# Three of eight gate groups per layer as seven block products, fed between 128-feature blocks

## The chip, the cores and the metric

The kernel runs on one core of a Trainium2 chip. The metric is device microseconds of one execution; lower is better. TensorE (PE) does the matrix products, VectorE (DVE) and ScalarE (ACT) the element-wise work, SyncE (SP) and GpSimd (POOL) issue transfers.

## The reference

Two layers of a decoder trunk over 256 positions of 2048 features. In each layer four branches (pooling, latent attention, gated convolution, cross-attention into memory) are projected to 2048 features and merged by sigmoid gates that are themselves a projection of the normed input `h`:

```python
proj = h @ w_in[l]
(pv, pz, cq, ckv, kr, mz, cb, cc, cx, cz, xq, xz, gpre) = jnp.split(proj, split_points, axis=-1)
y_pool = pool_mixer(pv, pool_w[l], pool_scale[l]) * jax.nn.silu(pz)
...
y_conv = conv_mixer(cb, cc, cx, conv_w[l]) * jax.nn.silu(cz)
...
gates = jax.nn.sigmoid((gpre + gate_b[l]).astype(jnp.float32)).astype(x.dtype).reshape(B, S, N_BRANCH, D_MODEL)
merged = gates[:, :, 0] * (y_pool @ w_branch[l, 0])
merged = merged + gates[:, :, 1] * (y_mla @ w_branch[l, 1])
...
x = x + merged @ w_out[l]
```

All arrays are float32. The gate projection `gpre` is 256 x 2048 times 2048 x 8192, in each layer.

## The kernel before

Every matrix operand is split into two float32r parts, `hi` (rounded) and `lo` (the rest), and a product is the sum of hi*hi, hi*lo and lo*hi. Weights come in chunks of 128 x 1024 numbers (512 KB): `wchunks` (L293) issues the transfer into `raw` on SP's queue (L303), ACT rounds it to `hi` (L304), DVE subtracts to get `lo` (L305). There are four buffers of `raw` and three each of `hi` and `lo`; `tc.high_priority(AHEAD)` puts these three steps ahead of other work that is ready.

Two loops use the chunks. `tm_block` (L308) holds 128 positions of an operand as the stationary side and streams 512 output features: twelve products of 512 columns a chunk (L317, L318, L319), 96 for a gate block of 512 features (K = 2048), into one two-bank `acc` tile. `fm_block` (L326) holds 128 features of the weights and streams the operand: its hi and lo parts together are 512 columns (L333), and the lo weights take 256 columns (L336). Its two 512-column results are added in halves by `fm_sum` (L339), an ACT copy and a DVE addition. PSUM has eight banks: three `acc` tiles of two, and two `ms` tiles of one.

The order inside a layer is written out by hand: attention first (`SEQUENCE`), then `gates` for the latent branch, the pooling branch, `gates` for memory, the convolution branch, and `gates` for pooling and convolution. `gates` (L809) goes over four blocks of 512 features: a gate block, bias (L818) and sigmoid (L819), the branch projection (48 products), multiplication (L825) and addition into `merged` (L826), which stays in on-chip memory for the whole layer. The pooling and convolution branches are `fm_block`s over `pv`, `pz`, `cc`, `cx`, `cb`, `cz` (256 features at a time), and DVE work between. The scheduler fixes each engine's order ahead of time and may put a later instruction that is ready ahead of one that waits.

Of the kernel before, what the change touches and what calls it, by code (L numbers as in the profile page):

```python
# [10 lines left out]
F32 = mybir.dt.float32  # L11
# [11 lines left out]
CK = 2  # L23
D = 2048
S = 256
DEPTH = 2
KT = D // P
# [33 lines left out]
def weight_plan():  # L61
# [7 lines left out]
    def fm(name):  # L69
        for b in range(4):  # L70
            add("in", OFF[name] + 256 * b, 256, 4, KT)

# [38 lines left out]
def tile_hybrid_trunk(  # L111
# [43 lines left out]
    x1d = ctx.enter_context(tc.tile_pool(name="dr", bufs=1, space=bass.MemoryType.DRAM)).tile([P, 2, D], F32, name="x1d")  # L155
# [170 lines left out]
    def fm_block(rhs, l, name, c0):  # L326
# [10 lines left out]
        return ps  # L337

# [160 lines left out]

    def silu_tile():  # L500
        return t4("z")[:, :1024].rearrange("p (n s) -> p n s", n=4)

    def silu_block(h, l, c0):
        z = silu_tile()
        for i in range(2):
            silu_half(z, i, h, l, c0)
        return z
# [226 lines left out]
    def pool_branch(l, vec, h):  # L734
        mixed = []
        for b in range(2):
            for i in range(2):
                ps = fm_block(h, l, "in", OFF["pv"] + 512 * b + 256 * i)
# [4 lines left out]
                fm_sum(v[:, :, 16:], ps)  # L743
# [35 lines left out]
    def conv_branch(l, vec, h):  # L779
        ys = []  # L780
        for b in range(2):
            cc = t4("cc")[:, :1024].rearrange("p (n s) -> p n s", n=4)
            for i in range(2):
                ps = fm_block(h, l, "in", OFF["cc"] + 512 * b + 256 * i)
                fm_sum(cc[:, 2 * i : 2 * i + 2, :], ps)
            u = t4("u")[:, :1032].rearrange("p (n s) -> p n s", n=4)
            nc.gpsimd.memset(u[:, :, :2], 0.0)
            for i in range(2):
                ps = fm_block(h, l, "in", OFF["cx"] + 512 * b + 256 * i)
                sl = slice(2 * i, 2 * i + 2)  # L790
                fm_sum(u[:, sl, 2:], ps)
# [8 lines left out]
            for i in range(2):  # L800
                ps = fm_block(h, l, "in", OFF["cb"] + 512 * b + 256 * i)
                sl = slice(2 * i, 2 * i + 2)
                fm_sum(bb[:, sl, :], ps)
                V.tensor_tensor(y[:, sl, :], y[:, sl, :], bb[:, sl, :], ALU.mult)
            sz = silu_block(h, l, OFF["cz"] + 512 * b)
# [3 lines left out]
    def gates(l, h, ys, branch, merged, first, last):  # L809
# [178 lines left out]
```

## Time and profile before

| | |
|---|---|
| median of 3 runs | 2513.04 us (2512.74 to 2514.82) |
| the profiled execution | 2512.52 us |
| its span in the trace | 2510.7 us |
| PE, PEld, DVE, ACT busy | 2498.8, 2110.1, 1538.0, 1249.1 us |
| bytes moved | 484.22 MB, mean 193 GB/s |

In the profile's rows a time is in microseconds unless marked ns; an `L` number is a line of the kernel, of a helper where several places share it; `out<-in` names tiles. A PE row's duration is the length of one product from start to drained end; products overlap, so the rate is read from the starts. PEld is the loading of the stationary side.

### The profile page before, as it was taken

Reading aid. Unit: us, or ns where it says so; the run is one execution under the profiler, and the core shown is the slowest. Engines: PE = TensorE matmul, PEld = TensorE weight load, DVE = VectorE, ACT = ScalarE, POOL = GpSimd, SP = SyncE. Lnnn points to the kernel's source line nnn. Section 1 sums busy time; section 2 is a strip of 40 time slices with the busy share of each in tenths; the row PEclk is TensorE's granted clock in tenths of the full one; section 3 lists DMA queues with packets and bytes.
Section 4 is the critical chain, followed back from the end, with each engine's and each line's share of the span. In section 5 each row is a group of like instructions: output and inputs, shape, how many; then the busy total and the mean of one; then the engine's idle time right before and its main releaser. Section 6 shows DMA issues by size and latency. Waiting matters only on the chain.

```text
span 2510.7 us, 32447 instructions
## 1 busy us (share of the span) xinstructions
PE 2498.8 (100%) x12402; PEld 2110.1 (84%) x12402; DVE 1538.0 (61%) x2132; ACT 1249.1 (50%) x1707; POOL 1.6 (0%) x16
## 2 busy tenths in 40 slices
PE   8999999999999999999999999999999999999999
PEld 7888888888888888888888888888888888888887
DVE  6767775566556665556474577755765566555554
ACT  7556674445444444445454566744444444444443
POOL 0000000000000000000000000000000000000000
PEclk9999999999999999999999999999999999999999
DMA  8665436655665566656655654366556655566565
GB/s 320 204 200 165 147 126 195 201 192 192 202 199 188 186 225 200 202 195 232 218 185 169 200 166 137 128 202 204 188 193 201 197 190 185 197 200 202 192 229 162
DMA packets 143677, 484.22 MB, mean 193 GB/s; under 512 B 16161, under 2 KB 17185, under 8 KB 143521
## 3 DMA queue, kind: packets, MB, share of 16 engines
q1 hardware_dynamic: 142800, 481.06, 58.9%
q8 instruction: 97, 1.59, 0.2%
q10 hardware_dynamic: 720, 1.09, 0.1%
q14 instruction: 60, 0.48, 0.1%
HBM read 477.89 MB, written 4.19 MB: 192 GB/s over the span
## 4 chain that ended last, share of the span: by engine, by line
PE 97%; DVE 1%; ACT 1%; DMA 0%; issue 0%; SPq 0%; DVEq 0%; ACTq 0%
PE acc L319 22%; PE acc L318 22%; PE acc L317 22%; PE acc L333 19%; PE acc L336 9%; PE ms L707 1%; PE ms L706 1%; PE ms L354 1%; DVE lo L305 0%; PE ms L555 0%; ACT hi L304 0%; PE ms L557 0%; PE ms L556 0%; PE acc L323 0%; DMA row<-in_x_dram 0%; PE ms L726 0%
## 5 line engine op out<-in xcount | busy, mean ns | idle before, releaser
L305 DVE TENSOR_TENSOR lo<-raw,hi 128x1024 fp32r<-128x1024 f32 (+2 forms) x884 | 1062.3, 1202 | 857.8 <-ACT hi L304 857.3
L304 ACT CAST hi<-raw 128x1024 fp32r<-128x1024 f32 (+2 forms) x884 | 914.6, 1035 | 1165.8 <-PE acc L319 794.4
L317 PE MATMUL acc<-hi,op 128*128 128x512 f32 (+2 forms) x2496 | 963.5, 386 | 5.6 <-ACT op L396 5.6
L318 PE MATMUL acc<-lo,op 128*128 128x512 f32 (+2 forms) x2496 | 959.3, 384 | 0.7 <-DVE lo L305 0.6
L319 PE MATMUL acc<-hi,op 128*128 128x512 f32 (+2 forms) x2496 | 958.9, 384 | 0.1
L333 PE MATMUL acc<-op,hi 128*128 128x512 f32 x2048 | 563.9, 396 | 0.0
L317 PEld LDWEIGHTS acc<-hi,op 128*128 128x128 f32 x2496 | 469.3, 188 | 93.9 <-ACT op L396 6.2
L318 PEld LDWEIGHTS acc<-lo,op 128*128 128x128 f32 x2496 | 469.5, 188 | 90.7 <-DVE lo L305 1.9
L319 PEld LDWEIGHTS acc<-hi,op 128*128 128x128 f32 x2496 | 469.1, 188 | 91.1 <-DVE op L397 0.7
L333 PEld LDWEIGHTS acc<-op,hi 128*128 128x128 f32 x2048 | 351.1, 189 | 47.9 <-issue 1.3
L336 PEld LDWEIGHTS acc<-op,lo 128*128 128x128 f32 x2048 | 314.8, 189 | 42.5
L336 PE MATMUL acc<-op,lo 128*128 128x256 f32 x2048 | 328.8, 282 | 0.0
L818 DVE TENSOR_TENSOR g<-acc,gb 128x1024 f32<-128x1024 f32 x32 | 39.2, 1224 | 12.7 <-PE acc L319 12.7
L341 ACT COPY fmt<-acc 128x512 f32<-128x512 f32 x72 | 41.5, 579 | 2.1 <-PE acc L336 2.1
L819 ACT ACTIVATE g<-g 128x1024 f32<-128x1024 f32 x32 | 34.0, 1062 | 6.7 <-DVE g L818 6.7
L825 DVE TENSOR_TENSOR g<-g,acc 128x1024 f32<-128x1024 f32 x24 | 29.3, 1222 | 9.9 <-PE acc L319 9.9
L826 DVE TENSOR_TENSOR merged<-merged,g 128x1024 f32<-128x1024 f32 x24 | 29.3, 1219 | 0.0
L498 DVE TENSOR_TENSOR z<-z,sg 128x512 f32<-128x512 f32 x32 | 22.1, 689 | 11.5 <-ACT sg L497 11.4
L197 ACT ACTIVATE junk<-acc 128x256 f32<-128x256 f32 (+2 forms) x68 | 25.3, 371 | 2.4 <-PE acc L319 1.5
L517 ACT ACTIVATE sm<-sm,smx,rqs 128x128 f32<-128x128 f32 (+1 forms) x32 | 17.3, 540 | 17.0 <-DVE smx L515 16.8
L497 ACT ACTIVATE sg<-z 128x512 f32<-128x512 f32 x32 | 20.2, 630 | 8.8 <-DVE z L342 8.6
L342 DVE TENSOR_TENSOR z<-acc,fmt 128x512 f32<-128x512 f32 x32 | 21.9, 684 | 1.6 <-ACT fmt L341 1.6
(197 smaller groups left out, 976.9 us busy)
## 6 DMA issues: line engine op xcount, KB each, us to landing
raw<-in_weights_dram SPq DMA_DIRECT2D x836, 512.0 KB, 4.0
raw<-in_weights_dram SPq DMA_DIRECT2D x32, 288.0 KB, 2.8
gb<-in_gate_b_dram SPq DMA_DIRECT2D x32, 256.0 KB, 4.2
raw<-in_weights_dram SPq DMA_DIRECT2D x16, 384.0 KB, 3.2
mt<-in_memT_dram SPq DMA_DIRECT2D x14, 256.0 KB, 6.0
row<-in_mem_dram SPq DMA_DIRECT2D x4, 512.0 KB, 8.4
row<-in_x_dram SPq DMA_DIRECT2D x4, 512.0 KB, 7.2
xt<-in_xT_dram SPq DMA_DIRECT2D x8, 256.0 KB, 5.6
```

What stands on the lines that cost most here:

```text
L304: A.copy(hi[:, :m], raw[:, :m])
L305: V.tensor_tensor(lo[:, :m], raw[:, :m], hi[:, :m].bitcast(F32), ALU.subtract)
L317: T.matmul(ps[:, t, :n], hh, hi[:, k, :], start=kk == 0, stop=False)
L318: T.matmul(ps[:, t, :n], hh, lo[:, k, :], start=False, stop=False)
L319: T.matmul(ps[:, t, :n], hl, hi[:, k, :], start=False, stop=kk == kt - 1)
L333: T.matmul(ps[:, j, :], hi[:, k, n0 : n0 + P], o, start=k0 + k == 0, stop=False)
L336: T.matmul(ps[:, j, :S], lo[:, k, n0 : n0 + P], o, start=False, stop=k0 + k == kt - 1)
L341: A.copy(tmp, ps[:, :, S:])
L818: V.tensor_tensor(g, pg, gb.unsqueeze(1).broadcast_to([P, 2, 512]), ALU.add)
L819: A.activation(g, g, AF.Sigmoid)
L825: V.tensor_tensor(g, g, pb, ALU.mult)
L826: V.tensor_tensor(mg, mg, g, ALU.add)
```

## The change

Of the eight pairs of gate blocks in a layer (four branches, two pairs of 1024 features), three, the two of pooling and the first of convolution (`SEVEN`), are computed by `seven`. It treats each of eight K slices of 256 as a 2 x 2 block product (two row halves of 128 positions, two K halves, two feature halves of 512) and forms seven block products from sums of blocks (Strassen's scheme, in Winograd's form) in place of eight; each is again three PE products of 512 columns. The seven results accumulate in seven PSUM banks, all three `acc` tiles and one `ms`, over the eight slices. The sums of operand blocks are made once per layer by `operand_sums`, the sums of weight blocks for every slice in place in `raw`, on DVE.

`seven` is a generator that yields after each product. `fine_block`, which takes the place of `fm_block` in the pooling and convolution branches, covers 128 features in one `ms` bank and first calls `pull(RATE)`, which runs on average 3.48 products of the stream (`RATE` = 160/46); the pooling projection pulls one product ahead of each of its results. The finished gates go to DRAM (`kept`) on POOL's queue and come back in `gates`. `merged` becomes four tiles in DRAM (`sums`), written and read on POOL's queue, since its buffer holds the operand sums. `hi` and `lo` get five buffers each, and the area for POOL's transfer descriptors shrinks. `gates` for memory now comes ahead of the pooling branch; pooling and convolution follow each other, with the stream between their blocks.

```diff
+SCRATCH = 1024
+FINE = ("pv", "pz", "cc", "cx", "cb", "cz")
 D = 2048
 S = 256
 DEPTH = 2
+SEVEN = [(0, 0), (0, 1), (2, 0)]
+RATE = (56 * len(SEVEN) - 8) / 46
...
     def fm(name):
-        for b in range(4):
-            add("in", OFF[name] + 256 * b, 256, 4, KT)
+        if name in FINE:
+            for b in range(8):
+                add("in", OFF[name] + 128 * b, 128, 8, KT)
+        else:
+            for b in range(4):
...
-            add("in", OFF["gate"] + bi * D + 512 * e, 512, 2, KT)
+            if (bi, e // 2) not in SEVEN:
+                add("in", OFF["gate"] + bi * D + 512 * e, 512, 2, KT)
+            elif e % 2 == 0:
+                add("in", OFF["gate"] + bi * D + 512 * e, 1024, 1, KT)
             add(f"br{bi}", 512 * e, 512, 2, 8)
...
+    dr = ctx.enter_context(tc.tile_pool(name="dr", bufs=1, space=bass.MemoryType.DRAM))
+    x1d = dr.tile([P, 2, D], F32, name="x1d")
+    sums = [dr.tile([P, 2, 512], F32, name=f"sums{e}") for e in range(4)]
+    kept = {(bi, 2 * ep + i): dr.tile([P, 2, 512], F32, name=f"kept{bi}{ep}{i}") for bi, ep in SEVEN for i in range(2)}
...
-            hi = wp.tile([P, 1024], F32R, tag="hi", name=nm("hi"), bufs=3)
-            lo = wp.tile([P, 1024], F32R, tag="lo", name=nm("lo"), bufs=3)
+            hi = wp.tile([P, 1024], F32R, tag="hi", name=nm("hi"), bufs=5)
+            lo = wp.tile([P, 1024], F32R, tag="lo", name=nm("lo"), bufs=5)
...
+    stream, owed = [], [0.0]
+
+    def pull(n):
+        owed[0] += n
+        while stream and owed[0] >= 1:
+            owed[0] -= 1
+            done = next(stream[0], True)
+            if done:
+                stream.pop(0)
+                break
+
...
+    def fine_block(rhs, l, c0):
+        pull(RATE)
+        ps = ms()
+        for k0, nk, kt, n, hi, lo in wchunks(l, "in", c0):
+            for k in range(nk):
+                o = rhs[(k0 + k) // 2][:, k % 2].rearrange("p a s -> p (a s)")
+                T.matmul(ps, hi[:, k, :], o, start=k0 + k == 0, stop=False)
+            for k in range(nk):
+                o = rhs[(k0 + k) // 2][:, k % 2, 0, :]
+                T.matmul(ps[:, :S], lo[:, k, :], o, start=False, stop=k0 + k == kt - 1)
+        return ps
+
+    def fine_sum(dst, ps):
+        tmp = t2("fmt")[:, :S]
+        A.copy(tmp, ps[:, S:])
+        V.tensor_tensor(dst, ps[:, :S], tmp, ALU.add)
+
...
+    def operand_sums(h, u, sx):
+        def run():
+            o = h[u]
+            w = t4("sw")
+            f = w[:, :512].rearrange("p (f s) -> p f s", f=4)
+            d = w[:, 512:1024].rearrange("p (f s) -> p f s", f=4)
+            a, b = slice(0, P), slice(P, S)
+            of = o.bitcast(F32)
+            V.tensor_tensor(d[:, 0:2, :], of[:, 0, :, b], of[:, 1, :, b], ALU.add)
+            V.tensor_tensor(d[:, 2:4, :], of[:, 0, :, a], of[:, 0, :, b], ALU.subtract)
+            V.tensor_tensor(f[:, 0:3:2, :], d[:, 0:3:2, :], d[:, 1:4:2, :], ALU.add)
+            V.tensor_tensor(f[:, 1, :], f[:, 0, :], of[:, 0, 0, a], ALU.subtract)
+            V.tensor_tensor(f[:, 1, :], f[:, 1, :], of[:, 0, 1, a], ALU.subtract)
+            V.tensor_tensor(f[:, 3, :], of[:, 1, 0, a], f[:, 1, :], ALU.subtract)
+            V.tensor_tensor(f[:, 3, :], f[:, 3, :], of[:, 1, 1, a], ALU.add)
+            q = sx[u // 4][:, u % 4]
+            A.copy(q[:, 0], f)
+            V.tensor_tensor(q[:, 1], f, q[:, 0].bitcast(F32), ALU.subtract)
+
+        return run
+
+    def seven(l, bi, ep, h, sx):
+        c0 = bi * D + 1024 * ep
+        off = plan["in", OFF["gate"] + c0][0]
+        a0, a1, a2, a3 = acc(), acc(), acc(), ms()
+        bank = {1: a0[:, 0, :], 6: a0[:, 1, :], 7: a1[:, 0, :], 5: a1[:, 1, :], 3: a2[:, 0, :], 2: a2[:, 1, :], 4: a3}
+        left, right = slice(0, 512), slice(512, 1024)
+        for u in range(8):
+            o, q = h[u], sx[u // 4][:, u % 4]
+            form = {
+                "A11": [o[:, 0, a, 0:P] for a in range(2)], "A12": [o[:, 1, a, 0:P] for a in range(2)],
+                "A22": [o[:, 1, a, P:S] for a in range(2)],
+            }
+            for i in range(4):
+                form[f"S{i + 1}"] = [q[:, a, i, :] for a in range(2)]
+
+            def product(i, name, pair, cols):
+                lh, (hi, lo) = form[name], pair
+                T.matmul(bank[i], lh[0], hi[:, cols], start=u == 0, stop=False)
+                T.matmul(bank[i], lh[0], lo[:, cols], start=False, stop=False)
+                T.matmul(bank[i], lh[1], hi[:, cols], start=False, stop=u == 7)
+
+            def pair():
+                hi = wp.tile([P, 1024], F32R, tag="hi", name=nm("hi"), bufs=5)
+                return hi, wp.tile([P, 1024], F32R, tag="lo", name=nm("lo"), bufs=5)
+
+            def lower(x, raw, cols):
+                V.tensor_tensor(x[1][:, cols], raw[:, cols], x[0][:, cols].bitcast(F32), ALU.subtract)
+
+            ra, rb = (wp.tile([P, 1024], F32, tag="raw", name=nm("raw"), bufs=4) for _ in range(2))
+            with tc.high_priority(AHEAD):
+                for i, r in enumerate((ra, rb)):
+                    at = off + P * 1024 * (2 * u + i)
+                    nc.sync.dma_start(r, weights[l, at : at + P * 1024].rearrange("(p m) -> p m", p=P))
+                x = pair()
+                A.copy(x[0][:, left], ra[:, left])
+                lower(x, ra, left)
+            product(1, "A11", x, left)
+            yield False
+            both = slice(0, 1024)
+            with tc.high_priority(AHEAD):
+                x = pair()
+                A.copy(x[0], rb)
+                V.tensor_tensor(ra[:, left], ra[:, right], ra[:, left], ALU.subtract)
+                V.tensor_tensor(ra[:, right], rb[:, right], ra[:, right], ALU.subtract)
+                lower(x, rb, both)
+            product(3, "S4", x, right)
+            yield False
+            product(2, "A12", x, left)
+            yield False
+            with tc.high_priority(AHEAD):
+                x = pair()
+                A.copy(x[0], ra)
+                V.tensor_tensor(rb[:, right], rb[:, right], ra[:, left], ALU.subtract)
+                V.tensor_tensor(rb[:, left], rb[:, right], rb[:, left], ALU.subtract)
+                lower(x, ra, both)
+            product(5, "S1", x, left)
+            yield False
+            product(7, "S3", x, right)
+            yield False
+            with tc.high_priority(AHEAD):
+                x = pair()
+                A.copy(x[0], rb)
+                lower(x, rb, both)
+            product(6, "S2", x, right)
+            yield False
+            product(4, "A22", x, left)
+            if u < 7:
+                yield False
+        c, u3 = t2("c"), t2("u3")
+        g = [t4("g")[:, :1024].rearrange("p (t c) -> p t c", t=2) for _ in range(2)]
+        A.copy(c, bank[1])
+        V.tensor_tensor(g[0][:, 0, :], c, bank[2], ALU.add)
+        V.tensor_tensor(c, c, bank[6], ALU.add)
+        V.tensor_tensor(u3, c, bank[7], ALU.add)
+        V.tensor_tensor(g[1][:, 1, :], u3, bank[5], ALU.add)
+        V.tensor_tensor(c, c, bank[5], ALU.add)
+        V.tensor_tensor(g[1][:, 0, :], c, bank[3], ALU.add)
+        V.tensor_tensor(g[0][:, 1, :], u3, bank[4], ALU.subtract)
+        for i in range(2):
+            gb = tp.tile([P, 512], F32, tag="gb", name=nm("gb"), bufs=2)
+            nc.sync.dma_start(gb, bcast_rows(gate_b[l, c0 + 512 * i : c0 + 512 * (i + 1)]))
+            V.tensor_tensor(g[i], g[i], gb.unsqueeze(1).broadcast_to([P, 2, 512]), ALU.add)
+            A.activation(g[i], g[i], AF.Sigmoid)
+            nc.gpsimd.dma_start(kept[bi, 2 * ep + i], g[i])
+        yield True
 
...
-                ps = fm_block(h, l, "in", OFF["pv"] + 512 * b + 256 * i)
                 g = 2 * b + i
                 w = WINDOWS[g]
                 v = t4("pv")[:, :544].rearrange("p (n s) -> p n s", n=2)
                 nc.gpsimd.memset(v[:, :, :16], 0.0)
-                fm_sum(v[:, :, 16:], ps)
+                fine_pair(v[:, :, 16:], h, l, OFF["pv"] + 512 * b + 256 * i)
...
-            sz = silu_block(h, l, OFF["pz"] + 512 * b)
+            sz = silu_fine(h, l, OFF["pz"] + 512 * b)
             (_, _, _, _, hi, lo), = wchunks(l, "pool", 512 * b)
             for i in range(2):
                 g = 2 * b + i
-                ps = acc()
+                y = t2("yp").rearrange("p (n s) -> p n s", n=2)
                 for j in range(2):
+                    pull(1)
+                    ps = ms().rearrange("p (o c) -> p o c", o=1)
                     for k in range(2):
-                        fm_tile(ps, j, hi, lo, mixed[g], k, 2 * i + k, j * P, k == 0, k == 1)
-                y = t2("yp").rearrange("p (n s) -> p n s", n=2)
-                fm_sum(y, ps)
+                        fm_tile(ps, 0, hi, lo, mixed[g], k, 2 * i + k, j * P, k == 0, k == 1)
+                    fine_sum(y[:, j, :], ps[:, 0, :])
...
-    def gates(l, h, ys, branch, merged, first, last):
+    def gates(l, h, ys, branch, first, last):
         bi = BRANCH_OF[branch]
         mT = []
         for e in range(4):
             c0 = bi * D + 512 * e
-            gb = tp.tile([P, 512], F32, tag="gb", name=nm("gb"), bufs=2)
-            nc.sync.dma_start(gb, bcast_rows(gate_b[l, c0 : c0 + 512]))
-            pg = tm_block(h, l, "in", OFF["gate"] + c0)
             g = t4("g")[:, :1024].rearrange("p (t c) -> p t c", t=2)
-            V.tensor_tensor(g, pg, gb.unsqueeze(1).broadcast_to([P, 2, 512]), ALU.add)
-            A.activation(g, g, AF.Sigmoid)
+            if (bi, e) in kept:
+                nc.gpsimd.dma_start(g, kept[bi, e])
+            else:
+                gb = tp.tile([P, 512], F32, tag="gb", name=nm("gb"), bufs=2)
+                nc.sync.dma_start(gb, bcast_rows(gate_b[l, c0 : c0 + 512]))
+                pg = tm_block(h, l, "in", OFF["gate"] + c0)
+                V.tensor_tensor(g, pg, gb.unsqueeze(1).broadcast_to([P, 2, 512]), ALU.add)
+                A.activation(g, g, AF.Sigmoid)
+            if not first:
+                mg = t4("mg")[:, :1024].rearrange("p (t c) -> p t c", t=2)
+                nc.gpsimd.dma_start(mg, sums[e])
             pb = tm_block(ys, l, f"br{bi}", 512 * e)
-            mg = merged[:, :, 512 * e : 512 * (e + 1)]
-            if first:
-                V.tensor_tensor(mg, g, pb, ALU.mult)
+            V.tensor_tensor(g, g, pb, ALU.mult)
+            if not first:
+                V.tensor_tensor(g, g, mg, ALU.add)
+            if last:
+                defer(transposed_operands(g, None, None, 4, mT), D_MT)
             else:
-                V.tensor_tensor(g, g, pb, ALU.mult)
-                V.tensor_tensor(mg, mg, g, ALU.add)
-            if last:
-                defer(transposed_operands(mg, None, None, 4, mT), D_MT)
+                nc.gpsimd.dma_start(sums[e], g)
         return mT
 
...
         y_mem = gated_out(o, sz)
-        merged = big.tile([P, 2, D], F32, tag="mm", name=f"merged{l}")
-        gates(l, h, y_mla, "mla", merged, True, False)
+        sx = [big.tile([P, 4, 2, 4, P], F32R, tag="mm", name=nm("sx")) for _ in range(2)]
+        background += [operand_sums(h, u, sx) for u in range(8)]
+        gates(l, h, y_mla, "mla", True, False)
+        gates(l, h, y_mem, "mem", False, False)
+        flush()
+        stream += [seven(l, bi, ep, h, sx) for bi, ep in SEVEN]
+        owed[0] = -RATE
         y_pool = pool_branch(l, vec, h)
-        gates(l, h, y_mem, "mem", merged, False, False)
         y_conv = conv_branch(l, vec, h)
-        gates(l, h, y_pool, "pool", merged, False, False)
-        mT = gates(l, h, y_conv, "conv", merged, False, True)
+        drain()
+        gates(l, h, y_pool, "pool", False, False)
+        mT = gates(l, h, y_conv, "conv", False, True)
...
-    nc = _bacc.Bacc("TRN2", target_bir_lowering=False, num_devices=1)
+    nc = _bacc.Bacc("TRN2", target_bir_lowering=False, num_devices=1, dynamic_dma_scratch_size=SCRATCH)
```

Not shown: `drain`, which runs what is left of the stream; `fine_pair` and `silu_fine`, which call `fine_block` twice and four times; and the same replacement of `fm_block` by `fine_pair` in the convolution branch.

More of the change, by code (lines that the diff above doesn't have):

```diff
@@ L69, in fm @@
     def fm(name):
-        for b in range(4):
-            add("in", OFF[name] + 256 * b, 256, 4, KT)
+        if name in FINE:
[3 more added lines that the diff above has]
+            for b in range(4):
+                add("in", OFF[name] + 256 * b, 256, 4, KT)
     for e in range(4):
@@ L154, in tile_hybrid_trunk @@
     plan, _ = weight_plan()
-    x1d = ctx.enter_context(tc.tile_pool(name="dr", bufs=1, space=bass.MemoryType.DRAM)).tile([P, 2, D], F32, name="x1d")
+    dr = ctx.enter_context(tc.tile_pool(name="dr", bufs=1, space=bass.MemoryType.DRAM))
+    x1d = dr.tile([P, 2, D], F32, name="x1d")
+    sums = [dr.tile([P, 2, 512], F32, name=f"sums{e}") for e in range(4)]
+    kept = {(bi, 2 * ep + i): dr.tile([P, 2, 512], F32, name=f"kept{bi}{ep}{i}") for bi, ep in SEVEN for i in range(2)}
     def load_vectors(l):
@@ L337, in fm_block, with drain @@
         return ps
+    stream, owed = [], [0.0]
[7 more added lines that the diff above has]
+                break
+    def drain():
+        while stream:
+            owed[0] = 1000.0
+            pull(0)
+        owed[0] = 0.0
+    def fine_block(rhs, l, c0):
[9 more added lines that the diff above has]
+        return ps
@@ new lines, in fine_sum, with fine_pair @@
+    def fine_sum(dst, ps):
+        tmp = t2("fmt")[:, :S]
+        A.copy(tmp, ps[:, S:])
+        V.tensor_tensor(dst, ps[:, :S], tmp, ALU.add)
+    def fine_pair(dst, h, l, c0):
+        for j in range(2):
+            fine_sum(dst[:, j, :], fine_block(h, l, c0 + 128 * j))
+    def operand_sums(h, u, sx):
[17 more added lines that the diff above has]
+        return run
@@ L498, in silu_half, with silu_fine @@
         V.tensor_tensor(z[:, sl, :], z[:, sl, :], sg, ALU.mult)
+    def silu_fine(h, l, c0):
+        z = silu_tile()
+        for i in range(2):
+            sl = slice(2 * i, 2 * i + 2)
+            fine_pair(z[:, sl, :], h, l, c0 + 256 * i)
+            sg = t2("sg").rearrange("p (n s) -> p n s", n=2)
+            A.activation(sg, z[:, sl, :], AF.Sigmoid)
+            V.tensor_tensor(z[:, sl, :], z[:, sl, :], sg, ALU.mult)
+        return z
     def silu_tile():
         return t4("z")[:, :1024].rearrange("p (n s) -> p n s", n=4)
[L503 to L507, printed above, removed]
     def softmax_rows(src, dst, spans, r, nr):
@@ L783, in conv_branch @@
             for i in range(2):
-                ps = fm_block(h, l, "in", OFF["cc"] + 512 * b + 256 * i)
-                fm_sum(cc[:, 2 * i : 2 * i + 2, :], ps)
+                fine_pair(cc[:, 2 * i : 2 * i + 2, :], h, l, OFF["cc"] + 512 * b + 256 * i)
             u = t4("u")[:, :1032].rearrange("p (n s) -> p n s", n=4)
@@ L788, in conv_branch @@
             for i in range(2):
-                ps = fm_block(h, l, "in", OFF["cx"] + 512 * b + 256 * i)
                 sl = slice(2 * i, 2 * i + 2)
-                fm_sum(u[:, sl, 2:], ps)
+                fine_pair(u[:, sl, 2:], h, l, OFF["cx"] + 512 * b + 256 * i)
                 V.tensor_tensor(u[:, sl, 2:], u[:, sl, 2:], cc[:, sl, :], ALU.mult)
@@ L800, in conv_branch @@
             for i in range(2):
-                ps = fm_block(h, l, "in", OFF["cb"] + 512 * b + 256 * i)
                 sl = slice(2 * i, 2 * i + 2)
-                fm_sum(bb[:, sl, :], ps)
+                fine_pair(bb[:, sl, :], h, l, OFF["cb"] + 512 * b + 256 * i)
                 V.tensor_tensor(y[:, sl, :], y[:, sl, :], bb[:, sl, :], ALU.mult)
-            sz = silu_block(h, l, OFF["cz"] + 512 * b)
+            sz = silu_fine(h, l, OFF["cz"] + 512 * b)
             ys += gated_out([y], [sz])
         return ys
-    def gates(l, h, ys, branch, merged, first, last):
+    def gates(l, h, ys, branch, first, last):
         bi = BRANCH_OF[branch]
```

## The prediction

> **What bounds the kernel now.** I read the page's engine line and chain first, then the waits of PE, then the rates of the two kinds of block in the timeline.
>
> ```profile
> span 2510.7 us, 32447 instructions
> ...
> PE 2498.8 (100%) x12402; PEld 2110.1 (84%) x12402; DVE 1538.0 (61%) x2132; ACT 1249.1 (50%) x1707; POOL 1.6 (0%) x16
> PE 97%; DVE 1%; ACT 1%; DMA 0%; issue 0%; SPq 0%; DVEq 0%; ACTq 0%
> ```
>
> ```profile
> PE acc L317 <- ACT op L396: 5.6, 1, 5.6
> PE acc L318 <- DVE lo L305: 0.6, 1, 0.6
> ```
>
> PE is on the chain for 97% of the span and waits 6.2 us in all. A busy PE could still be slow, so the starts count:
>
> ```profile
> 600.15 0.39 PE L317 MATMUL acc<-hi,op 128*128 128x512 f32 x1
> ...
> 602.87 0.39 PE L317 MATMUL acc<-hi,op 128*128 128x512 f32 x1
> ```
>
> Twelve products (three lines, four times) lie between these: 2.72/12 = 0.2267 us for a product of 512 columns, the same through the stage. Fewer products, with all else hidden, means less time at that rate. For the blocks that hold the weights, and for how a result leaves PSUM, there is one stretch:
>
> ```profile
> 507.76 1.09 PE L333 MATMUL acc<-op,hi 128*128 128x512 f32 x4
> ...
> 508.69 0.63 PE L336 MATMUL acc<-op,lo 128*128 128x256 f32 x4
> 508.89 1.05 ACT L304 CAST hi<-raw 128x1024 fp32r<-128x1024 f32 x1 [1.76 <-PE acc L333]
> ...
> 509.16 1.09 PE L333 MATMUL acc<-op,hi 128*128 128x512 f32 x4
> 509.84 0.58 ACT L341 COPY fmt<-acc 128x512 f32<-128x512 f32 x1
> 509.97 1.23 DVE L305 TENSOR_TENSOR lo<-raw,hi 128x1024 fp32r<-128x1024 f32 x1 [1.58 <-ACT hi L304]
> ...
> 510.56 1.09 PE L333 MATMUL acc<-op,hi 128*128 128x512 f32 x4
> 511.11 0.68 DVE L342 TENSOR_TENSOR pv<-acc,fmt 128x512 f32<-128x512 f32 x1
> 511.90 0.72 DVE L749 TENSOR_TENSOR ps<-pv 128x542 f32<-128x542 f32 x1
> ```
>
> Four K tiles of 128 features take 509.16 - 507.76 = 1.40 us, so a block of 128 features (16 K tiles) takes 5.6 us. The block that ended at 508.69 + 0.63 = 509.32 was out of PSUM at 511.79, 2.47 us later: 0.52 until ACT was free, the copy, 0.69 until DVE was free, the addition. Now that is hidden by three `acc` tiles.
>
> **The change, part by part.** *Products.* A pair of gate blocks has 2 x 96 = 192 products; `seven` has 8 slices x 7 x 3 = 168 of the same shape. 24 x 0.2267 = 5.44 us for a pair, six pairs in two layers: **32.6 us** off PE. PE gets nothing new, as the 128-feature blocks have the same products as before. Against the profiled execution, 2512.5 (0.5 under the median), the floor is 2512.5 - 32.6 = 2479.9.
>
> *DVE in the mixed stage.* Pooling and convolution with the stream between them take PE 48 x 5.6 + 5.6 (pooling projections) + 168 x 0.227 x 3 = 389 us in a layer. DVE has there what it has now, plus the stream's work:
>
> ```profile
> core 0: us, PE busy (x) PEld busy (x) DVE busy (x) ACT busy (x) POOL busy (x), PEclk, DMA share, GB/s
> 498.00:593.30 95.30, 95.30 (x545) 83.35 (x544) 65.68 (x76) 45.49 (x54) 0.23 (x2) 1.00 0.59 188
> 593.30:723.90 130.60, 130.60 (x578) 108.23 (x577) 74.73 (x67) 57.24 (x57) 0.10 (x1) 1.00 0.64 201
> 723.90:903.50 179.60, 179.60 (x1025) 157.09 (x1024) 109.27 (x122) 77.84 (x86) 0.00 (x0) 1.00 0.57 188
> ```
>
> ```profile
> L305 DVE TENSOR_TENSOR lo<-raw,hi 128x1024 fp32r<-128x1024 f32 x836 | 1022.7, 1224 | 822.6 <-ACT hi L304 822.2
> ...
> L342 DVE TENSOR_TENSOR z<-acc,fmt 128x512 f32<-128x512 f32 x32 | 21.9, 684 | 1.6 <-ACT fmt L341 1.6
> ...
> L661 ACT COPY kn<-acc 128x256 f32<-128x256 f32 x16 | 5.9, 371 | 0.0
> ...
> L729 DVE TENSOR_TENSOR yf<-ms,z 128x256 f32<-128x256 f32 x16 | 6.7, 421 | 7.2 <-PE ms L727 7.1
> ```
>
> Now 65.7 + 109.3 = 175 us. A slice adds three subtractions of 1024 columns, one of 512 and four sums of 512: 3 x 1.224 + 5 x 0.684 = 7.1 us, times 24 = 170. A pair's end has seven additions of 512 and two of 1024, 7.2 us, times three = 22. Together 367 of 389, 94%. Back to back they cost less: the 1.23 us of 509.97 lets the next start 1.14 later, so 219 new instructions may save 0.09 each, which gives 347, 89%. DVE fits, barely, where it has 64% now; at 60 to 80 us it was busy throughout and PE with it. ACT adds 3.7 us a slice (three casts of 1.05, a half) to 123 of 389 and is far from full. I charge nothing for DVE; what covers it are five `hi` and `lo` buffers, about 10 us of PE's work ahead. Gone, it costs the excess of DVE over PE (second rival).
>
> *Handover of the one free bank.* `seven` holds all `acc` tiles and one `ms`, so each 128-feature block writes the same bank that the last one must have left. With 256 columns the way out is 0.52 + 0.371 + 0.69 + 0.421 = 2.00 us after the modelled end, 2.16 after PE could go on (509.16, not 509.32). The cover is three products (2.04) or four (2.72); between pooling projections one (0.68). Uneven gaps can be evened out, since PE's order puts later products into a wait:
>
> ```profile
> 263.40 0.27 PE L722 MATMUL ms<-cst,sm 128*128 128x128 f32 x1
> 263.43 0.42 PE L317 MATMUL acc<-hi,op 128*128 128x384 f32 x1
> ...
> 264.87 0.70 PE L726 MATMUL ms<-pT,mw 128*128 128x256 f32 x2
> ```
>
> Here L726 waits for an ACT copy of L722's bank and seven products of another block fill 1.4 us. So totals count: 55 handovers x 2.16 = 119 us in a layer against 168 x 0.68 = 114 of products. Short by 5, in two layers **10 us**. Ends: 0 where ACT and DVE are free at once (0.95 + 0.16 us each), and over 60 us a layer with one more 1.14 us subtraction ahead of each; I take the row's own waits, the nearest.
>
> *Change of pair.* Four times in the kernel a new pair needs the banks of the old. The second product's bank is free after the copy and six additions, 0.52 + 0.58 + 0.69 + 6 x 0.79 (the step from 511.11 to 511.90, one using the other's result) = 6.5 us, against a block and a product, 5.6 + 0.68 = 6.3. Two subtractions for the block's chunks in between make it 8.8. Ends 0 and 2.5; I take 1, **4 us**.
>
> *Transfers.* SP's order of weights has a new limit: two of four `raw` buffers stay in a slice's hands, the two others must carry two chunks in 5.6 + 3.48 x 0.68 = 8.0 us.
>
> ```profile
> SPq L303 <- DVE lo L305: 1855.0, 811, 9.6
> ```
>
> ```profile
> raw<-in_weights_dram SPq DMA_DIRECT2D x836, 512.0 KB, 4.0
> ```
>
> ```profile
> 0.00:10.00 10.00, 4.25 (x8) 2.27 (x8) 3.38 (x6) 5.41 (x8) 0.20 (x4) 1.00 0.81 277
> ...
> 10.00:20.00 10.00, 9.92 (x44) 8.21 (x45) 8.83 (x16) 7.81 (x14) 0.00 (x0) 1.00 1.02 398
> ...
> 60.00:80.00 20.00, 20.00 (x94) 16.62 (x93) 20.00 (x41) 14.96 (x24) 0.00 (x0) 1.00 0.81 292
> ```
>
> SP waits for DVE to release a buffer even now; landing 4.0, cast 1.05 and subtraction 1.14 are 6.2 us, under 8.0, so nothing. A slice's next transfer stands in SP's order ahead of later blocks' chunks, and these wait with it. In the pooling gates a block of 10.9 us (48 products) needs four chunks, a kept gate, a sum in and a sum out, 3.67 MB, 337 GB/s; 398 was reached. Nothing; at the 292 of the last row, 7 us in two layers. POOL has 36 more transfers a layer; a write behind its addition holds up later reads there, but each read has a block's 10.9 us against 4.0. Nothing, at the most 2 us at each read that comes late.
>
> *Operand sums.* Eight times some 3.6 us of DVE (four forms of 128, at most 0.421 like the 256, three of 256, one of 512) = 29 us in 130.6 us of gates where DVE has 74.7 now: hidden. The additions into `merged` only change their target: nothing. The new order of memory gates and pooling: nothing on PE.
>
> Sum: 2479.9 + 10 + 4 = **2494 us**.
>
> **A rule weighed.** The first wait above is 5.6 us long, in the stretch 0 to 10 us, and the granted clock there is 1.00. The Trainium skill, TensorE: Matmul & The Clock Gate, "The HAM clock gate (the 'warmup' mystery)", has the array fall to half clock after an idle window of about 3.4 us. By that rule each change of pair that waited longer would cost some 1.7 us more, and 2494 would become 2501; the trace's row shows no such drop, and my waits are shorter, so it gets no term and a chance of 0.02, inside my case.
>
> **The rivals.** *Handover is the bound.* If each of 110 handovers in two layers is late by 0.3 us beyond the products, the 32.6 us are gone; at 0.6, 2479.9 + 66 = 2546. For it: only one bank, and a DVE at 90% rarely is free at once. Against: PE's order is filled as shown, and before a copy waits only the rest of one cast. Slower: 0.14. *DVE is the bound.* If most of its some 440 instructions in a layer's mixed stage wait for the one before as at 511.90 (0.79 in place of 0.60), 347 becomes 431, 42 over PE in each layer: 2564. It decides from 0.13 us each. Most neighbours are independent: 0.08. *The gain is used up*, the handover at 0.25 to 0.35 us each: 2508 to 2518, 0.12. *Transfers bind in the pooling gates*: 2494 + 7 = 2501, inside my own case.
>
> **How the numbers follow.** My case, 2480 to 2508, has 0.66 (its own 8 in 10: 2481 to 2506). Some 0.2% (5 us) is what can be told from no change here, so same has 0.12, slower 0.22. The range from the floor 2479 to 2528 leaves out the worse half of the two slower rivals and little below.
>
> **What would show it.** Right: 144 products fewer at 0.227 us; DVE near 90% in the mixed stages; PE's waits there for the `ms` bank some 5 us a layer, and 1 us at a change of pair. Wrong: PE waiting for `lo` or `hi` in the stream (DVE or `raw` buffers), for `fmt` additions in over half the blocks, or in the pooling gates for weights with DMA share near 1.

## The result and the profile after

The changed kernel took 2581.4 us (median of 4 runs, 2578.6 to 2583.2) against 2513.9 for the kernel before on the same chip: a ratio of 1.0266 [1.0248, 1.0284]. It is slower, and 53 us above the predicted range's upper end.

From the page of the profile, engine line and chain of the changed kernel:

```profile
span 2581.4 us, 33256 instructions
...
PE 2511.1 (97%) x12258; PEld 2091.0 (81%) x12258; DVE 1799.0 (70%) x2646; ACT 1338.9 (52%) x1881; POOL 40.5 (2%) x88
...
PE 88%; DVE 6%; DMA 2%; ACT 2%; issue 1%; SPq 0%; DVEq 0%; ACTq 0%
```

12258 matmuls are the 144 fewer that were meant. But PE is on the chain for 88% of the span instead of 97%. The two mixed stages and, third, a stretch of the pooling gates in windows (busy us by engine, then granted clock, DMA share, GB/s):

```profile
629.80:1066.00 436.20, 407.48 (x2049) 335.70 (x2048) 351.07 (x444) 221.67 (x273) 4.85 (x13) 0.97 0.57 189
1904.00:2354.00 450.00, 422.26 (x2113) 347.98 (x2112) 360.60 (x456) 227.09 (x280) 4.85 (x13) 0.97 0.57 188
1100.00:1150.00 50.00, 50.00 (x230) 41.38 (x229) 34.87 (x32) 21.94 (x23) 3.85 (x8) 1.00 0.85 314
```

The pooling gates run at full PE with transfers at 314 GB/s. All the loss is in the mixed stages: 436 us for the first instead of 389, with DVE busy 351 us, the amount that was predicted, yet idle for 85 us of it. PE's waits, as (total us, times, longest):

```profile
PE acc L429 <- ACT hi L446: 15.3, 12, 2.7
PE acc L430 <- DVE lo L438: 13.3, 17, 2.2
PE ms L376 <- DVE z L385: 7.0, 10, 1.8
PE ms L337 <- DVE yp L385: 6.5, 6, 1.8
PE acc L429 <- ACT hi L473: 6.4, 6, 1.3
```

With each matmul's distance to the next start, less 0.2267 or 0.1238 us, the two stages have 70 us of waiting, 24 us of half clock and 8 us of small delays more than the columns need (before: 0.7 in all). 102 - 32.6 = 69, and the span grew by 70.7.

By name most of the waiting is for `hi` and `lo` in the stream, which I had written down as the sign of a late DVE or of missing `raw` buffers. One such place shows more. The timeline of the changed kernel:

```profile
682.73 0.37 ACT L384 COPY fmt<-ms 128x256 f32<-128x256 f32 x1
...
683.21 1.22 DVE L319 TENSOR_TENSOR lo<-raw,hi 128x1024 fp32r<-128x1024 f32 x1
...
684.34 0.69 DVE L916 SCALAR_TENSOR_TENSOR ps<-ps,pv 128x512 f32<-128x512 f32 x1
...
684.94 2.36 DVE L438 TENSOR_TENSOR lo<-raw,hi 128x1024 fp32r<-128x1024 f32 x2
...
686.19 1.46 SPq L444 DMA_DIRECT2D raw<-in_weights_dram  x2
...
687.21 0.68 DVE L505 TENSOR_TENSOR op<-ps,op 128x512 fp32r<-128x512 f32 x1
...
687.82 2.36 DVE L319 TENSOR_TENSOR lo<-raw,hi 128x1024 fp32r<-128x1024 f32 x2
...
688.41 0.39 PE L431 MATMUL ms<-hi,op 128*128 128x512 f32 x1
...
690.09 0.42 DVE L385 TENSOR_TENSOR pv<-ms,fmt 128x256 f32<-128x256 f32 x1
690.88 0.62 ACT L446 CAST hi<-raw 128x512 fp32r<-128x512 f32 x1 [1.96 <-DMA raw<-in_weights_dram]
...
691.55 0.59 PE L429 MATMUL acc<-hi,op 128*128 128x512 f32 x1 [2.75 <-ACT hi L446]
...
691.94 0.63 PE L376 MATMUL ms<-op,hi 128*128 128x512 f32 x1
```

The block's last matmul ends at 682.5 and ACT's copy at 683.10. The addition (L385) that gives the bank back starts at 690.09, after 7 us of other DVE work that stands ahead of it in DVE's order: three subtractions of blocks, two of the stream, and steps of the pooling. Until 688.6 PE works through 24 matmuls of the stream; then these need the next slice, whose transfer was issued only at 686.19, behind the same DVE work, which held its `raw` buffer. PE's 2.75 us are booked to the cast, but the next block could not have run either: its bank came back at 690.51.

Over all 112 copies and additions of the trace, the way from where PE could go on after the last matmul to the end of the addition has a median of 1.89 us, under my price of 2.16; but 18 of them took 6.5 to 10.4 us, and the mean is 2.91. The mean's excess over the median, times 112, is some 114 us. This is a correlation; the experiments had to show that it is the cause.

The clock is the other find. Here are three windows of 3.4 us around the wait:

```profile
685.00:688.40 3.40, 3.16 (x13) 2.14 (x13) 3.40 (x5) 2.42 (x4) 0.00 (x0) 1.00 0.71 214
688.40:691.80 3.40, 0.65 (x3) 0.25 (x2) 2.38 (x4) 1.14 (x2) 0.00 (x0) 1.00 0.92 363
691.80:695.20 3.40, 3.40 (x9) 2.63 (x9) 1.80 (x3) 0.00 (x0) 0.00 (x0) 0.50 0.58 194
```

PE was idle for 2.75 of 3.4 us, and for the next 3.4 us its granted clock is 0.50.

### The profile page after: what moved, and what is told of

Read it like the earlier page. It is cut to its first block, busy times and chain, and to the rows that moved or that the text cites. A ratio compares the mean times of both kernels' runs of the same rounds, so it can differ in the third digit from the quotient of the medians.

```text
span 2581.4 us, 33256 instructions
## 1 busy us (share of the span) xinstructions
PE 2511.1 (97%) x12258; PEld 2091.0 (81%) x12258; DVE 1799.0 (70%) x2646; ACT 1338.9 (52%) x1881; POOL 40.5 (2%) x88
## 3 DMA queue, kind: packets, MB, share of 16 engines
q8 instruction: 96, 1.57, 0.2%
## 4 chain that ended last, share of the span: by engine, by line
PE 88%; DVE 6%; DMA 2%; ACT 2%; issue 1%; SPq 0%; DVEq 0%; ACTq 0%
PE acc L333 18%; PE acc L332 18%; PE acc L331 18%; PE ms L376 13%; PE ms L379 6%; PE acc L347 4%; PE acc L350 2%; DVE lo L319 2%; DMA raw<-in_weights_dram 2%; PE acc L430 2%; PE acc L429 2%; PE acc L431 2%; DVE lo L438 1%; ACT hi L318 1%; PE ms L870 1%
## 5 line engine op out<-in xcount | busy, mean ns | idle before, releaser
L319 DVE TENSOR_TENSOR lo<-raw,hi 128x1024 fp32r<-128x1024 f32 (+1 forms) x788 | 942.6, 1199 | 579.7 <-ACT hi L318 572.3
L318 ACT CAST hi<-raw 128x1024 fp32r<-128x1024 f32 (+1 forms) x788 | 812.1, 1033 | 879.9 <-PE acc L333 586.5
L331 PE MATMUL acc<-hi,op 128*128 128x512 f32 (+2 forms) x2112 | 812.5, 385 | 6.0 <-ACT op L555 5.7
L333 PE MATMUL acc<-hi,op 128*128 128x512 f32 (+2 forms) x2112 | 808.5, 383 | 0.5 <-DVE op L556 0.5
L376 PE MATMUL ms<-op,hi 128*128 128x512 f32 x1536 | 400.6, 404 | 10.6 <-DVE z L385 7.0
L376 PEld LDWEIGHTS ms<-op,hi 128*128 128x128 f32 x1536 | 289.8, 195 | 79.2 <-DVE z L385 10.8
L379 PE MATMUL ms<-op,lo 128*128 128x256 f32 x1536 | 214.7, 283 | 0.0
L347 PE MATMUL acc<-op,hi 128*128 128x512 f32 x512 | 144.3, 397 | 0.0
L347 PEld LDWEIGHTS acc<-op,hi 128*128 128x128 f32 x512 | 87.6, 189 | 11.7 <-issue 0.7
L350 PEld LDWEIGHTS acc<-op,lo 128*128 128x128 f32 x512 | 78.5, 189 | 10.7 <-issue 0.7
L350 PE MATMUL acc<-op,lo 128*128 128x256 f32 x512 | 83.8, 283 | 0.0
```

The source lines that it names most:

```text
L318: A.copy(hi[:, :m], raw[:, :m])
L319: V.tensor_tensor(lo[:, :m], raw[:, :m], hi[:, :m].bitcast(F32), ALU.subtract)
L331: T.matmul(ps[:, t, :n], hh, hi[:, k, :], start=kk == 0, stop=False)
L333: T.matmul(ps[:, t, :n], hl, hi[:, k, :], start=False, stop=kk == kt - 1)
L347: T.matmul(ps[:, j, :], hi[:, k, n0 : n0 + P], o, start=k0 + k == 0, stop=False)
L350: T.matmul(ps[:, j, :S], lo[:, k, n0 : n0 + P], o, start=False, stop=k0 + k == kt - 1)
```

## The experiments

Theories at the start: **D**, DVE has too much work in the mixed stage; **R**, the two `raw` buffers that a slice holds make transfers late; **H**, the one free `ms` bank comes back too late. A floor of 2513.9 - 32.6 = 2481 is what the fewer products alone would give; the changed kernel is 100 us over it.

**Without the stream.** `SEVEN = []`: no pair by seven products, the rest of the change stays.

> No pair is computed by seven products (all eight by the plain blocks); the 128-feature blocks, the sums in DRAM, the five hi and lo buffers and the new order stay. Every theory puts the loss into the stream, so about the time before, 2508 to 2520. Above 2525: the rest of the change costs too. PE's waits in the pooling and convolution stages should be near zero, as two ms banks are free.

2524.9 us, ratio 1.0044 [1.0029, 1.0059], above the range expected. So the rest costs 11 us. In its timeline the pooling projections wait:

```profile
699.52 1.22 DVE L319 TENSOR_TENSOR lo<-raw,hi 128x1024 fp32r<-128x1024 f32 x1 [1.57 <-ACT hi L318]
...
700.67 0.42 DVE L385 TENSOR_TENSOR z<-ms,fmt 128x256 f32<-128x256 f32 x1
...
701.14 0.49 PE L337 MATMUL ms<-op,hi 128*128 128x512 f32 x1 [1.11 <-DVE z L385]
```

Even with two `ms` banks free, one subtraction ahead of an addition stops PE, because a projection is only 0.7 us long.

**Without the sums of weight blocks.** The four `V.tensor_tensor` of `ra` and `rb` in `seven` are gone.

> Leaves out the four sums of weight blocks of every slice (the products then use the blocks as they are). DVE has 66 us less in each layer's mixed stage. Theory D (DVE is late with its work, and hi, lo and the handover wait for it): 2490 to 2520, and no half-clock stretches. Theory R (the two raw buffers that a slice keeps make the next slice's first transfer late): the buffers are held as long, 2560 to 2580, with PE still waiting for the first cast of a slice. Theory H (one bank for all 128-feature blocks): 2560.

2521.9 us, 1.0039 [1.0025, 1.0053], 59 us less than the changed kernel and 2 past D's range. I took this for D. It says only that this work does harm where it stands; a later run shows why.

**Buffers.** `bufs=` of `raw`, and of `hi` and `lo`: 6 and 4; 4 and 4; 4 and 3 (the change has 4 and 5).

> Six raw buffers in place of four, paid for by four hi and four lo in place of five. Theory R: the first cast of a slice is no longer waited for, about 10 us a layer of waits and most of the half-clock stretches (12 us a layer) go: 2530 to 2550, and clearly below the run with four raw and four hi and lo. Theory D: no better than that run.

> Four hi and four lo in place of five, four raw as in the changed kernel: the control of the run with six raw. Theory D: less work ahead, 2590 to 2620. Theory R: raw binds first, within 10 us of 2581.

> The changed kernel with three hi/lo buffers, as before the change, instead of five. Theory D (DVE's own load of some 350 us a layer is too near to PE's 389, whatever the buffers): a shorter cover makes PE wait at least as long as with four, 2563 to 2590. Theory O (DVE executes in a written order, and a subtraction that the plan puts far ahead stands at its head, waiting for a cast or for PE to give back a buffer, while the addition that PE needs is behind it; the 83 us of DVE's idle time in the 436 us of the first mixed stage are this): fewer buffers mean less work placed far ahead, so the step from four to three goes on in the direction of five to four, 2540 to 2562, with DVE's idle time at the stream's subtractions under the 37.3 us of four buffers.

2560.8 us, 1.0188 [1.0173, 1.0204]; 2562.8 us, 1.0202 [1.0187, 1.0217]; 2601.0 us, 1.0347 [1.0330, 1.0364]. Two more `raw` buffers bring 2 us: R falls. The number of `hi` and `lo` has no direction (2581, 2563, 2601 for 5, 4, 3), which contradicts O (the theory of DVE's order in the text of the last run) as well as a simple D. My reading, not shown by a run of its own: each number gives another order of the work on DVE, and some orders are luckier.

**The sums on GpSimd.**

```diff
-                V.tensor_tensor(ra[:, left], ra[:, right], ra[:, left], ALU.subtract)
+                nc.gpsimd.tensor_tensor(ra[:, left], ra[:, right], ra[:, left], ALU.subtract)
```

and the three others alike.

> The changed kernel with the four sums of weight blocks on GpSimd instead of VectorE. They are 2.7 us of VectorE in a slice, 64 us a layer. Theory D: without them on VectorE the time falls towards that of the kernel that left them out (2522), 2520 to 2540, as GpSimd is idle and a slice has some 17 us. Rival L (not DVE's load counts, but the length of the chain transfer, cast, sum, sum, cast, subtraction in a slice, with the raw buffers held through it): on a slower engine the chain gets longer, and the time stays at 2560 to 2600.

2611.6 us, 1.0387 [1.0371, 1.0402]: slower by 30, above the ranges of D and of L. Its engine line, and then groups from 629 to 1060 us (count, then busy us and mean ns):

```profile
PE 2509.7 (96%) x12258; PEld 2093.9 (80%) x12258; DVE 1818.4 (70%) x2454; ACT 1339.3 (51%) x1881; POOL 353.3 (14%) x280
```

```profile
L465 POOL TENSOR_TENSOR raw<-raw 128x512 f32<-128x512 f32 x24 | 47.1, 1964 | 1.9
```

```profile
L953 DVE TENSOR_TENSOR u<-u,cc 128x512 f32<-128x512 f32 x4 | 6.3, 1565 | 0.1
```

```profile
L385 DVE TENSOR_TENSOR pv<-ms,fmt x8: 410/416/419, 636.9 to 699.8; 128x256 f32<-128x256 f32 x8
```

A sum takes 1.3 to 2.0 us in the mean instead of 0.69, and many of DVE's own instructions are longer in this kernel: L953 in the changed kernel is

```profile
L953 DVE TENSOR_TENSOR u<-u,cc 128x512 f32<-128x512 f32 x4 | 2.7, 682 | 0.0
```

The additions that read PSUM keep their 0.42. The Trainium skill, GPSIMD Engine Reference, "1. Specifications", says that GpSimd shares its SBUF interfaces with DVE and contends with instructions that have two SBUF inputs; these rows agree.

So the run doesn't test D: DVE has 192 instructions less and is busy no less, 1818 us for 1799.

**Two pairs, four pairs.** `SEVEN` with two and with four entries. The rate follows, so a block has 2.3, 3.5 or 4.7 products of three matmuls as cover.

> The changed kernel with two pairs of gate blocks in a layer by seven products instead of three (SEVEN has (0,0) and (0,1); the rate follows by its formula). 48 products a layer less to gain for the third pair, so 10.9 us less gain; but VectorE has 64 us less work in the mixed stage, 287 of 351 us, 82%. Theory D: the loss of 101 us over the floor falls more than in proportion, 2525 to 2545. Rival H (the handover of the one bank): 110 handovers remain with 2.3 products as cover instead of 3.4, so they get longer; 2565 to 2600.

> The changed kernel with four pairs a layer instead of three, and the handover as the change has it. With two pairs (2.3 products as cover) the loss over the floor was 143 us, with three (3.4) 101. H: with 4.7 products the loss goes on falling, to some 60 over a floor of 2469, 2515 to 2550. D: DVE's load passes PE's, 2600 to 2680.

2635.3 us, 1.0481 [1.0465, 1.0497], and 2587.9 us, 1.0294 [1.0280, 1.0307]. With two pairs DVE has 64 us a layer less to do, and the kernel is 54 us slower: D can't give that. H named the direction, not the size. With two pairs PE's waits for the bank are 50 us or more in all (19 in the changed kernel), while the largest single row is still one for `lo`:

```profile
PE acc L430 <- DVE lo L438: 16.9, 18, 2.6
PE ms L376 <- DVE z L385: 14.5, 16, 1.8
PE ms L337 <- DVE yp L385: 12.9, 8, 2.3
PE ms L376 <- DVE u L385: 9.6, 8, 1.8
PE ms L376 <- DVE cb L385: 9.4, 12, 1.7
```

Over their floors two, three and four pairs lose 143, 100 and 118 us: less cover below three; above three neither forecast held, and both effects may be in it.

**The addition left out.** `fine_sum` is one copy of the first half.

```diff
-        A.copy(tmp, ps[:, S:])
-        V.tensor_tensor(dst, ps[:, :S], tmp, ALU.add)
+        A.copy(dst, ps[:, :S])
```

> The changed kernel with the way out of the one ms bank cut down: a block of 128 features leaves PSUM by one ACT copy of its first 256 columns; the DVE addition of the two halves is left out (the part from the low halves of the operands is missing). VectorE has 56 additions of 0.42 us less in a layer, 23 us against 64 for the weight sums. Theory D alone: in proportion to the 59 us that the weight sums brought, some 21 us, 2560. Theory H (handover of the bank behind DVE's queue): PE's waits for ms, 19 us in both layers, go as well, and so does what the late banks set back in the stream: 2520 to 2545.

2496.9 us, 0.9926 [0.9909, 0.9943]: 84 us less, more than either forecast, for 23 us a layer of DVE's work. The sums, 64 us a layer, had brought 59.

**The addition off the handover.** This keeps the whole computation and all of DVE's work:

```diff
-        tmp = t2("fmt")[:, :S]
-        A.copy(tmp, ps[:, S:])
-        V.tensor_tensor(dst, ps[:, :S], tmp, ALU.add)
+        tmp = t2("fmt")
+        A.copy(tmp, ps)
+        V.tensor_tensor(dst, tmp[:, :S], tmp[:, S:], ALU.add)
```

> The changed kernel, whole, with one line of the way out of the ms bank different: ACT copies all 512 columns (0.58 us instead of 0.37) and DVE adds the two halves out of SBUF, so the bank is free after the copy and the addition may come when it likes. DVE has the same number of additions as in the changed kernel. Theory H (PE waits because the one bank comes back only behind what stands in DVE's queue): near the 2497 of the kernel without additions, plus some 0.2 us for a part of the 110 handovers, 2495 to 2515. Theory D (DVE's load): nothing gained, 2570 to 2590.

Below this is the short way out, and the changed kernel's own, through DVE, the long one. 2519.1 us, 1.0016 [1.0008, 1.0025]: 62 us less than the changed kernel, 4 us past the range of H. The page and the timeline at the place shown above:

```profile
PE 2481.2 (99%) x12258; PEld 2085.7 (83%) x12258; DVE 1789.8 (71%) x2646; ACT 1365.7 (54%) x1881; POOL 40.5 (2%) x88
```

```profile
684.40 0.58 ACT L384 COPY fmt<-ms 128x512 f32<-128x512 f32 x1
...
686.95 1.98 PE L376 MATMUL ms<-op,hi 128*128 128x512 f32 x8
...
690.31 0.42 DVE L385 TENSOR_TENSOR pv<-fmt 128x256 f32<-128x256 f32 x1
```

DVE has as many instructions and as many busy microseconds as in the changed kernel (1790 and 1799), and the addition still comes late, 5.3 us after the copy (7.0 in the changed kernel). But the next block starts 2.0 us after the copy. In DVE's waits the same holds; first the changed kernel, then this one:

```profile
DVE lo L438 <- PE ms L379: 26.4, 23, 1.5
```

```profile
DVE lo L438 <- PE ms L379: 35.3, 26, 1.5
```

DVE still stands with a stream subtraction at its head; the addition behind it no longer holds the bank. H is shown for these 62 us: the harm is in the place of the addition.

**The same edit in other settings.** With four pairs, and with four `hi` and `lo` buffers:

> The kernel e9_copy_both with four pairs of gate blocks a layer by seven products instead of three; 10.9 us fewer products, 224 of them between the same 46 blocks and 10 others. H: the handover has 4.7 products as cover and stays off the path, so the gain is kept, 2485 to 2505, if DVE can follow. D: DVE has 175 + 4 x 64 = 431 us or more in a mixed stage of 427 us of PE, so PE waits for lo and hi in the stream; 2530 to 2600.

> The kernel e9_copy_both with four hi/lo buffers instead of five. With the handover as the change has it, four buffers were 19 us faster than five. H: that came from subtractions placed ahead of the additions in DVE's order; with the addition off the handover it no longer matters, so the two are within 8 us of each other. If the number of buffers counts by itself (the stream's own cover), the 19 us come again, or the sign turns and it is over 8 us slower.

2542.1 us, 1.0110 [1.0097, 1.0123]: 46 less than four pairs with the long way out, but above three pairs, so the gain of the fourth isn't kept. D's range held here and H's did not, so with four pairs DVE's work may count again. Yet PE waits there for ACT's copies and for DVE's additions at a change of pair, and little for `lo`:

```profile
PE ms L376 <- ACT fmt L384: 13.2, 8, 3.5
PE ms L337 <- ACT fmt L384: 11.0, 9, 3.0
PE acc L429 <- DVE c L487: 10.5, 4, 3.9
...
PE acc L430 <- DVE lo L438: 1.9, 2, 1.1
```

The cause of this loss stays open.

With four buffers it is 2525.8 us, 1.0041 [1.0028, 1.0054]: 37 less than with the long way, and 7 more than five, where four had been 19 better. In three settings so far the short way out gains, 62, 46 and 37 us, so one lucky order can't be the reason.

**What is left: the projections.** `pull(3)` in place of `pull(1)` and 24 in place of 8 in `RATE`; with the short way out, then with six `raw` and four `hi` and `lo` buffers besides, then with the long way.

> The kernel e9_copy_both with three products instead of one ahead of each of the eight pooling projections of a layer, and 3.13 instead of 3.48 ahead of each block. In e9_copy_both the waits from 725 to 785 us, where the projections lie, sum to some 10 us and two of the half-clock windows lie there, 13 us a layer. Theory H: they are handovers with 0.68 us of cover; with 2.04 us most of it goes, 2494 to 2508, and the kernel is faster than before the change. Rival M (the mixed stage has some 35 us of waiting in any order, from raw buffers, casts and DVE's work, and it only moves): 2512 to 2522.

> The kernel e13_copy_pull3 with six raw and four hi/lo buffers instead of four and five. In e9_copy_both PE once a layer waits 3.1 us behind an ACT that waits 5.6 us for a transfer (at 916 us), and a half-clock window follows; with two raw buffers more that transfer is issued earlier. R: 8 to 12 us faster than e13_copy_pull3. H: raw buffers change nothing, as they changed 2 us in the kernel with the long handover; within 6 us.

> The changed kernel with three products instead of one ahead of each pooling projection, and 3.13 instead of 3.48 ahead of each block; the way out through DVE as the change has it. H: the projections' waits (some 11 us in both layers, with half clock) go, while 46 blocks a layer have 0.08 us less cover: 2560 to 2578. Rival: the gaps even out over the whole stage by PE's order, so only the sum of the products counts, 2578 to 2588.

2516.9 us, 1.0010 [1.0001, 1.0018]; 2519.4 us, 1.0021 [1.0012, 1.0029]; 2608.6 us, 1.0368 [1.0353, 1.0382]. The projections' waits went, and waits elsewhere came: M, the rival, holds. `raw` buffers change nothing here either. Alone the edit makes it 27 us slower, which neither forecast had; the short way out is worth 92 us in this setting.

**No stream, short way out.** `SEVEN = []` and the copy of both halves.

> The kernel e1_no_stream (no pair by seven products, all else of the change, 2525) with the way out of e9_copy_both. Its loss of 11 us against before was put down to the pooling projections, which wait for the bank behind DVE's additions. H: with the addition off the way most of the 11 us goes, 2514 to 2519. Rival: the loss is the change's other part (the gates in another order, the sums of the branches through DRAM), 2522 to 2527.

2521.3 us, 1.0026 [1.0014, 1.0037], between the two forecasts. Only 4 of the 11 us went. Its span is 8.0 us over that of before, and its PE starts have 7.2 us of waits in the two mixed stages that were not there before, all at the projections:

```profile
PE ms L337 <- ACT fmt L384: 5.1, 4, 1.3
```

**DVE's part in the rest.** The short way out and `pull(3)`, with the addition on GpSimd (`nc.gpsimd.tensor_tensor(dst, ...)`), and with the sums of weight blocks left out instead.

> The kernel e13_copy_pull3 with the addition of the two halves, out of SBUF, on GpSimd instead of DVE; nothing left out. DVE has 56 additions of 0.42 us less in a layer, the same as in e8_no_additions (2497). Theory D (what is left of the loss is DVE's load): 2494 to 2506, faster than before the change. Theory C (contention): in e6_pool_sums a sum of 512 columns took GpSimd 1.3 to 2.0 us, and DVE's own instructions beside it were longer (512 columns 1.55 us instead of 0.68, the 1024 of a block's subtraction 1.43 instead of 1.22 in the mean); additions of 256 columns then hold DVE up for about as long as they relieve it, 2512 to 2530.

> The kernel e13_copy_pull3 without the four sums of weight blocks (left out, so three of the seven products in a slice use other weights than they should); DVE has 64 us a layer less. e13_copy_pull3 has 37 us over the floor of 2480. D: with DVE far from full most of these go, 2483 to 2496. Rival: they are waits for casts and buffers in the order as written, whatever DVE's load, 2505 to 2517.

2512.7 us, 0.9994 [0.9985, 1.0003], as C (contention) had it: no measurable difference to the kernel before, for 144 products fewer. An addition takes GpSimd three times DVE's 0.42:

```profile
L385 POOL TENSOR_TENSOR z<-fmt 128x256 f32<-128x256 f32 x16 | 22.2, 1389 | 89.8 <-ACT fmt L384 81.5 <-issue 8.2
```

Without the sums: 2515.2 us, 1.0001 [0.9993, 1.0010]. 64 us a layer less on DVE bring 2 us here, 59 with the long way out. With three pairs D falls: the sums did harm because they stood ahead of additions that PE waited for. This kernel has 34 us over the floor; the starts in its trace show some 33, about 22 as waits, 7 as half clock and 4 as small delays. Its largest waits:

```profile
PE ms L376 <- ACT fmt L384: 7.1, 6, 1.5
PE acc L429 <- ACT hi L469: 7.1, 2, 3.6
```

The second is one place in each layer, a slice's last cast, with windows of half clock behind it. Which order of ACT's work would free these was not tried. The kernel without additions comes 18 us lower; it differs in the shorter copy and in its `pull` too, so that part is not settled.

## Why the prediction was wrong

**Products:** right. 144 fewer, in pooling gates and elsewhere at the old rate; the 32.6 us are there.

**Handover:** this step failed. It named the right resource and both ends ("over 60 us a layer with one more 1.14 us subtraction ahead of each"), and then took the near end, 10 us in two layers, from a row where one cast and one subtraction stood ahead. With the stream, DVE's order held 7.0 us ahead of the addition shown above, and up to 9.4 at others. Taking the addition off the way brought 62 us, 0.56 for each of 110 handovers; the rival that was given 0.14 had 0.6 each and 66 us. The argument that "totals count" failed with it: PE did fill in 24 matmuls, but what it filled in ran dry, because the next slice's weights came through the same DVE queue. Of the 100 us over the floor, these 62 are shown to be the handover; the 38 that stay with the short way out are waits and half clock whose cause is open in part.

**DVE's load:** the amount was right (351 us of 347 to 367), "I charge nothing" was not, though not by the rival's way. A load near 90% of PE's 389 us meant long stretches of work ahead of any one urgent instruction; the five buffers cover the stream's own subtractions, not an addition behind them. The share itself was not the bound: 64 us less changed 2 us once the additions were off the path (three pairs).

**Clock:** given no term. Fifteen windows in the mixed stages of the changed kernel cost some 24 us, four in the kernel with the short way out some 6. The evidence against the rule was misread. The trace of the kernel before has no record of the clock ahead of 9.7 us, so the 1.00 of the row from 0 to 10 us says nothing of the time right after the first wait. The starts do:

```profile
7.51 0.63 PE L317 MATMUL acc<-hi,op 128*128 128x512 f32 x1
7.93 0.63 PE L318 MATMUL acc<-lo,op 128*128 128x512 f32 x1
8.36 0.63 PE L319 MATMUL acc<-hi,op 128*128 128x512 f32 x1
```

They are 0.43 us apart, as in the changed kernel's window of half clock from 691.8 us on, and not 0.2267: after the wait of 5.6 us PE ran at half its rate. So the rule was right in kind, and shorter waits than it names were enough (below).

**Projections:** not priced beyond eight of the handovers. They are 7 to 11 us without any stream.

**Change of pair:** PE waits 1.2 us for `c` in both layers, under my 4; the pair's seven additions, though, are among what stood ahead of the longest handovers, 10.4 us. **Transfers, pooling gates, new order of the gates:** nothing, as said; the kernel without stream loses at the projections alone. The prediction's 7 us at 292 GB/s is one layer's; for two it should have been some 14.

## What to carry to other kernels

When one buffer must come back to the bottleneck engine, price its return by what the releasing engine's queue holds ahead of that instruction at the worst places, not by its median or its busy share; if two engines are on the way, let the one with the shorter queue do all that frees the buffer (37 to 92 us in the four settings here). A wait booked to one operand may hide that another came hardly earlier, so look a few microseconds back for the instruction that everything queued behind. Work that is moved to an idle engine must be timed there and beside its neighbours first.

## Unexpected of the hardware

The half clock lasts 3.413 us, or a whole number of these, and in the mixed stages begins only on a grid of that step (691.8, 743.0, 787.4 us and so on in the changed kernel). It followed windows in which PE's idle time summed to some 2 of 3.4 us, in several waits as well as in one. I count 0.2267 us of work from the start of a product of 512 columns, and the rest as idle. Over the mixed stages of the changed kernel and of the 18 runs, none of 4323 full-clock windows with less than 2.0 us of idle time was then followed by half clock, 25 of 41 with 2.0 to 2.2 us were, and all 94 with more. The Trainium skill, TensorE: Matmul & The Clock Gate, "The HAM clock gate (the 'warmup' mystery)", speaks of an idle window of about 3.4 us; the step agrees, but these traces show that part of one is enough.

GpSimd's sum of 512 columns took 1.3 to 2.0 us in the mean. In that kernel DVE's L953, 512 columns with both inputs in SBUF, went from 0.68 to 1.57 us, but not every such line did: L916 stayed at 0.69.
